# A gated broadcast on one core: gates and x swap their load queues, the first store waits for its tile alone, and one of its tokens is multiplied in one instruction

## The chip, the cores and the metric

The kernel runs on one core of a Trainium2 chip. The metric is device time in microseconds, lower is better. The engines that matter are DVE (the vector engine), ACT (the scalar engine), SP (the sync engine, which here only issues transfers) and the core's 16 DMA engines. Transfers issued by SP stand in one queue (q1 in the profile), those issued by ACT in another (q10); both are served by the same 16 DMA engines.

## The reference

```python
# x: 8 x 256 x 512 float32; gate_weights: 8 x 256 x 8 float32
gate_weights = gate_weights / (np.sum(gate_weights, axis=-1, keepdims=True) + 1e-8)
output = x[:, :, None, :] * gate_weights[:, :, :, None]     # 8 x 256 x 8 x 512
```

Every token's 512 values are written eight times, once for each expert, each time scaled by that expert's normalised gate. 4.26 MB are read, 33.55 MB are written.

## The kernel before, in words

The 2048 tokens are laid over 128 partitions, 16 tokens (numbered j = 0 to 15) on each, so that a partition's tokens are contiguous in memory. Everything that is read fits in the chip's memory: `g_all` holds all gates, `x_all` all of x. The products go to `ring`, which has ten slots of one token by eight experts (16 KB per partition), and from there to memory in five stores. `CHUNKS` lists them as (first token, tokens, first slot): two tokens, three, three, four, four.

Loads: SP issues the head of x (tokens 0 to 3, line 67), the body (tokens 4 to 12, line 69) and, after the entry barrier, the rest (tokens 13 to 15, line 73). ACT issues the gates (line 68). `issue_before_entry_barrier` moves the first three ahead of the barrier that all engines pass at the start, by placing them at the head of their engine's instructions.

Gates: four small DVE operations (lines 78 to 81) sum the gates, add the small constant, take the reciprocal and multiply, giving `gn`. ACT does a small copy first (line 76), so that its table is loaded early.

Products: `scale_one` makes one expert of one token, 512 elements per partition, on ACT (line 88) or DVE (line 90). `scale_token` makes all eight experts of a token in one DVE instruction (line 93), with x and the gates broadcast. Tokens 0 and 1 are split three experts to ACT and five to DVE, token 2 is all ACT's, token 3 two to ACT and six to DVE; of the later chunks the first token is ACT's, the others are whole tokens on DVE. Token 4 is a whole token too.

Stores: SP issues each store (line 118) once the tile's products are there. The first has one more wait, for the landing of the body load, put in by `add_manual_dep`. A slot that is used again waits for the store that read it.

Of the kernel before, what the change touches and what calls it, by code (L numbers as in the profile page):

```python
# [1 line left out]

# [4 lines left out]

SLOTS = 10
HEAD = 4
TAIL = 13  # L10
CHUNKS = ((0, 2, 0), (2, 3, 2), (5, 3, 5), (8, 4, 0), (12, 4, 6))


def issue_before_entry_barrier(nc, loads):
    names = [bi.ins.name for bi in loads]

    def move(nc):
        blocks = nc.main_func.blocks
        entry = blocks[0].instructions
        moved = []  # L20
        for block in blocks[1:]:
            for ins in list(block.instructions):
                if ins.name in names:
                    block.instructions.remove(ins)
                    moved.append(ins)
        assert sorted(i.name for i in moved) == sorted(names)
        for ins in reversed(moved):
            at = next(k for k, other in enumerate(entry) if other.engine == ins.engine)
            entry.insert(at, ins)

    nc.at_finalize(move)


@with_exitstack
def kernel(
    ctx: ExitStack,
    tc: tile.TileContext,
    x: bass.AP,
    gate_weights: bass.AP,
    out: bass.AP,  # L40
):
    nc = tc.nc
    P = 128

    B, S, D = x.shape
    E = gate_weights.shape[-1]
    J = B * S // P

    fp32 = mybir.dt.float32
    mult = mybir.AluOpType.mult  # L50

    x_v = x.flatten_outer_dims().rearrange("(p j) d -> p j d", p=P)
    g_v = gate_weights.flatten_outer_dims().rearrange("(p j) e -> p j e", p=P)
    out_v = out.rearrange("b s e d -> (b s) e d").rearrange(
        "(p j) e d -> p j e d", p=P
    )

    pool = ctx.enter_context(tc.tile_pool(name="pool", bufs=1))

    g_all = pool.tile([P, J, E], fp32)  # L60
    x_all = pool.tile([P, J, D], fp32)
    ring = pool.tile([P, SLOTS, E, D], fp32)
    gsum = pool.tile([P, J, 1], fp32)
    gn = pool.tile([P, J, E], fp32)
    warm = pool.tile([P, 1], fp32)

    first_load = nc.sync.dma_start(out=x_all[:, 0:HEAD, :], in_=x_v[:, 0:HEAD, :])  # L67
    gate_load = nc.scalar.dma_start(out=g_all, in_=g_v)
    body_load = nc.sync.dma_start(
        out=x_all[:, HEAD:TAIL, :], in_=x_v[:, HEAD:TAIL, :]  # L70
    )
    issue_before_entry_barrier(nc, [first_load, gate_load, body_load])
    nc.sync.dma_start(out=x_all[:, TAIL:J, :], in_=x_v[:, TAIL:J, :])

    nc.vector.memset(warm, 0.0)  # L75
    nc.scalar.copy(out=warm, in_=warm)  # L76

    nc.vector.reduce_sum(out=gsum, in_=g_all, axis=mybir.AxisListType.X)  # L78
    nc.vector.tensor_scalar_add(out=gsum, in0=gsum, scalar1=1e-8)  # L79
    nc.vector.reciprocal(out=gsum, in_=gsum)  # L80
    nc.vector.tensor_tensor(  # L81
        out=gn, in0=g_all, in1=gsum.to_broadcast([P, J, E]), op=mult
    )

    def scale_one(engine, j, e, slot):
        o_ap, s_ap = ring[:, slot, e, :], gn[:, j, e : e + 1]
        if engine is nc.scalar:
            nc.scalar.mul(out=o_ap, in_=x_all[:, j, :], mul=s_ap)  # L88
        else:
            nc.vector.tensor_scalar_mul(out=o_ap, in0=x_all[:, j, :], scalar1=s_ap)  # L90

    def scale_token(j, slot):
        nc.vector.tensor_tensor(  # L93
            out=ring[:, slot, :, :],
            in0=x_all[:, j : j + 1, :].to_broadcast([P, E, D]),
            in1=gn[:, j, :].unsqueeze(2).to_broadcast([P, E, D]),
            op=mult,
        )

    for j0, m, s0 in CHUNKS:  # L100
        for i in range(m):
            j, slot = j0 + i, s0 + i
            if j < 2:
                for e in range(E):
                    on_act = e < 3
                    scale_one(nc.scalar if on_act else nc.vector, j, e, slot)
            elif j == 2:
                for e in range(E):
                    scale_one(nc.scalar, j, e, slot)
            elif j == 3:  # L110
                for e in range(E):
                    scale_one(nc.scalar if e < 2 else nc.vector, j, e, slot)
            elif i == 0:
                for e in range(E):
                    scale_one(nc.scalar, j, e, slot)
            else:
                scale_token(j, slot)
        store = nc.sync.dma_start(  # L118
            out=out_v[:, j0 : j0 + m, :, :], in_=ring[:, s0 : s0 + m, :, :]
        )  # L120
        if j0 == 0:
            tc.add_manual_dep(
                store.ins,
                body_load.ins.name,
                mybir.DependencyInfo(
                    mybir.DependencyClass.Sync, mybir.DependencyReason.DATA
                ),
                reason="no store among the loads",
            )


# [1 line left out]
_INS = ['x', 'gate_weights']  # L133
_OUTS = [((8, 256, 8, 512), 'float32')]


# [23 lines left out]
```

## Time and profile before

| | us |
|---|---|
| median of 7 runs | 92.31 (92.25 to 92.43) |
| profiled execution, its own time | 92.25 |
| its span, first to last instruction | 90.5 |
| DVE busy | 46.6 |
| ACT busy | 26.3 |
| first store issued | 10.58 |
| first products begun (ACT and DVE) | 6.28 |

In the profile a row of the timeline gives start and duration in us, the engine (SPq and ACTq are the issuing sequencers), the line of the kernel, the operation, the tile written and the tiles read, a count, and in brackets the idle time before it with what ended it. A row of the groups by shape gives a count, then busy us and the mean ns of one, then the idle time before them. A row of a DMA queue gives packets, MB and the time that the packets took as a share of 16 engines over the window asked for. In the row of slices each digit is the busy share of a fortieth of the span, in tenths.

### The profile page before, as it was taken

How to read it: one execution, taken by the hardware profiler on the slowest of the kernel's cores; microseconds unless marked ns; L12 is line 12 of the kernel's file. 1: busy time of each engine (PE TensorE's matmuls, PEld its weight loads, DVE VectorE, ACT ScalarE, POOL GpSimd, SP SyncE). 2: the span in 40 equal slices, each digit the busy share in tenths (PEclk: the TensorE clock that was granted, in tenths of full speed). 3: DMA queues.
4: the chain of work that ended last, by engine and by line, in shares of the span. 5: the costliest groups of instructions: out<-in, count | busy, mean ns of one | idle time of the engine just before them, and what ended most of it. 6: DMA issues, size and time to landing. Idle time of an engine off the chain costs nothing.

```text
span 90.5 us, 140 instructions
## 1 busy us (share of the span) xinstructions
DVE 46.6 (52%) x30; ACT 26.3 (29%) x42; POOL 0.2 (0%) x4
## 2 busy tenths in 40 slices
DVE  0069999999999999999990495000000000000000
ACT  4229999995990000000000498000000000000000
POOL 0000000000000000000000000000000000000000
DMA  5999999999898889888988999999999955999990
GB/s 127 454 434 399 405 529 464 464 391 420 348 696 348 348 348 696 348 348 348 696 348 348 464 464 464 464 464 464 464 464 464 464 232 232 464 464 464 464 464 0
DMA packets 1296, 37.81 MB, mean 418 GB/s; under 512 B 144, under 2 KB 272, under 8 KB 400
## 3 DMA queue, kind: packets, MB, share of 16 engines
q1 hardware_dynamic: 1152, 37.75, 97.3%
q10 hardware_dynamic: 144, 0.07, 0.2%
HBM read 4.26 MB, written 33.55 MB: 418 GB/s over the span
## 4 chain that ended last, share of the span: by engine, by line
DMA 52%; ACT 9%; ACTq 1%; SPq 0%; issue 0%
DMA out_dram<-ring 41%; DMA x_all<-in_x_dram 11%; ACT ring L88 9%; ACTq L155 1%; SPq L67 0%; ACTq L88 0%; SPq L118 0%
## 5 line engine op out<-in xcount | busy, mean ns | idle before, releaser
L93 DVE TENSOR_TENSOR ring<-x_all,gn 128x4096 f32<-128x4096 f32 x9 | 39.2, 4419 | 3.7 <-DMA out_dram<-ring 3.7
L88 ACT ACTIVATE ring<-x_all,gn 128x512 f32<-128x512 f32 x40 | 24.8, 708 | 28.5 <-DMA out_dram<-ring 25.0
L90 DVE TENSOR_SCALAR ring<-x_all,gn 128x512 f32<-128x512 f32 x16 | 6.4, 481 | 0.0
L78 DVE TENSOR_REDUCE gsum<-g_all 128x16 f32<-128x128 f32 x1 | 0.3, 286 | 3.8 <-DMA g_all<-in_gate_weights_dram 3.8
L76 ACT ACT_TABLE_LOAD x1 | 1.3, 1283 | 1.2 <-PEq L144 1.2
L75 DVE MEMSET warm<- 128x1 f32 x1 | 0.1, 59 | 1.3 <-PEq L144 1.3
L81 DVE TENSOR_TENSOR gn<-g_all,gsum 128x128 f32<-128x128 f32 x1 | 0.3, 293 | 0.0
L80 DVE RECIPROCAL gsum<-gsum 128x16 f32<-128x16 f32 x1 | 0.3, 253 | 0.0
L76 ACT COPY warm<-warm 128x1 f32<-128x1 f32 x1 | 0.2, 191 | 0.0
L79 DVE TENSOR_SCALAR gsum<-gsum 128x16 f32<-128x16 f32 x1 | 0.2, 176 | 0.0
L144 POOL MEMSET const-bfloat16-1.0<- 128x1 bf16 x1 | 0.1, 103 | 0.0
L144 POOL MEMSET const-uint8-127<- 128x1 uint8 x1 | 0.1, 102 | 0.0
L144 POOL MEMSET const-float32-0.0<- 128x1 f32 x1 | 0.1, 100 | 0.2 <-issue 0.2
L144 POOL MEMSET const-float32-1.0<- 128x1 f32 x1 | 0.1, 99 | 0.0
## 6 DMA issues: line engine op xcount, KB each, us to landing
out_dram<-ring SPq DMA_DIRECT2D x2, 6144.0 KB, 22.3
out_dram<-ring SPq DMA_DIRECT2D x1, 4096.0 KB, 11.5
x_all<-in_x_dram SPq DMA_DIRECT2D x1, 2304.0 KB, 10.1
x_all<-in_x_dram SPq DMA_DIRECT2D x1, 1024.0 KB, 4.9
x_all<-in_x_dram SPq DMA_DIRECT2D x1, 768.0 KB, 11.1
g_all<-in_gate_weights_dram ACTq DMA_DIRECT2D x1, 64.0 KB, 5.0
out_dram<-ring SPq DMA_DIRECT2D x2, 28.2
```

Source lines behind the costliest of these rows:

```text
L75: nc.vector.memset(warm, 0.0)
L76: nc.scalar.copy(out=warm, in_=warm)
L78: nc.vector.reduce_sum(out=gsum, in_=g_all, axis=mybir.AxisListType.X)
L79: nc.vector.tensor_scalar_add(out=gsum, in0=gsum, scalar1=1e-8)
L80: nc.vector.reciprocal(out=gsum, in_=gsum)
L81: nc.vector.tensor_tensor(out=gn, in0=g_all, in1=gsum.to_broadcast([P, J, E]), op=mult)
L88: nc.scalar.mul(out=o_ap, in_=x_all[:, j, :], mul=s_ap)
L90: nc.vector.tensor_scalar_mul(out=o_ap, in0=x_all[:, j, :], scalar1=s_ap)
L93: nc.vector.tensor_tensor(out=ring[:, slot, :, :], in0=x_all[:, j : j + 1, :].to_broadcast([P, E, D]), in1=gn[:, j, :].unsqueeze(2).to_bro ...
L144: nc = _bacc.Bacc("TRN2", target_bir_lowering=False, num_devices=1)
L155: with _tile.TileContext(nc) as tc:
```

## The change

The gates are issued by SP and are its first instruction. x comes in two loads (tokens 0 to 3, tokens 4 to 15) that ACT issues; all three are ahead of the barrier. Token 0 is one whole-token multiply on DVE; token 1 is split four experts to ACT and four to DVE (before: three and five for each of both tokens). The first store no longer waits for a load, only for its tile. Products of all other tokens, the chunks and the slots are as they were. On DVE the whole-token multiply of token 0 stands ahead of the one-expert multiplies of tokens 1 and 3.

```diff
-    first_load = nc.sync.dma_start(out=x_all[:, 0:HEAD, :], in_=x_v[:, 0:HEAD, :])
-    gate_load = nc.scalar.dma_start(out=g_all, in_=g_v)
-    body_load = nc.sync.dma_start(
-        out=x_all[:, HEAD:TAIL, :], in_=x_v[:, HEAD:TAIL, :]
-    )
-    issue_before_entry_barrier(nc, [first_load, gate_load, body_load])
-    nc.sync.dma_start(out=x_all[:, TAIL:J, :], in_=x_v[:, TAIL:J, :])
+    first_load = nc.scalar.dma_start(out=x_all[:, 0:HEAD, :], in_=x_v[:, 0:HEAD, :])
+    gate_load = nc.sync.dma_start(out=g_all, in_=g_v)
+    last_load = nc.scalar.dma_start(out=x_all[:, HEAD:J, :], in_=x_v[:, HEAD:J, :])
+    issue_before_entry_barrier(nc, [first_load, gate_load, last_load])
...
-            if j < 2:
+            if j == 0:
+                scale_token(j, slot)
+            elif j == 1:
                 for e in range(E):
-                    on_act = e < 3
-                    scale_one(nc.scalar if on_act else nc.vector, j, e, slot)
+                    scale_one(nc.scalar if e < 4 else nc.vector, j, e, slot)
...
-        store = nc.sync.dma_start(
+        nc.sync.dma_start(
             out=out_v[:, j0 : j0 + m, :, :], in_=ring[:, s0 : s0 + m, :, :]
         )
-        if j0 == 0:
-            tc.add_manual_dep(
-                store.ins,
-                body_load.ins.name,
-                mybir.DependencyInfo(
-                    mybir.DependencyClass.Sync, mybir.DependencyReason.DATA
-                ),
-                reason="no store among the loads",
-            )
```

More of the change, by code (lines that the diff above doesn't have):

```diff
@@ L9 @@
 HEAD = 4
-TAIL = 13
 CHUNKS = ((0, 2, 0), (2, 3, 2), (5, 3, 5), (8, 4, 0), (12, 4, 6))
```

## The prediction

> **What bounds the kernel now.** I read the busy shares over time first, because they say whether any engine is the limit, then the chain that ended last, then the edges of the transfer stream. The page of the kernel before:
>
> ```profile
> span 90.5 us, 140 instructions
> DVE 46.6 (52%) x30; ACT 26.3 (29%) x42; POOL 0.2 (0%) x4
> ...
> DMA  5999999999898889888988999999999955999990
> ```
>
> The compute engines are half idle; the DMA engines are full from the second slice to the last but one. (The two 5s are large packets counted where they start: in the packet records the 16 engines are all occupied there.) By those records the first packet starts at 1.00 us and the last ends at 89.26 us, with no hole between. The time is thus 1.00 us of start, 88.26 us of transfer, 1.2 us until the last landing has been seen and the program ended, and 92.25 - 90.5 = 1.75 us around the span. The chain in order of time shows where this stream could break:
>
> ```profile
> 0.42 10.06 DMA x_all<-in_x_dram
> 10.49 0.02 issue
> 10.50 0.03 SPq L118
> 10.53 0.05 issue
> 10.58 11.49 DMA out_dram<-ring
> ```
>
> The first store is issued at 10.58, 0.09 us after the body of x has landed, and not because its tile is late: of the compute before it, DVE's ten multiplies end at 6.28 + 9 x 0.397 + 0.48 = 10.33 and ScalarE's six at 6.28 + 5 x 0.614 + 0.71 = 10.06. The last piece of x, issued at 1.25 us, lands 11.1 us later, at 12.35. So store packets stand in the queue before the loads run out: the first starts at 11.56, 0.98 us after its issue, and engine by engine stores follow loads (mean over the 16 engines 11.77, last 11.94). From there to the end of the last packet there are 77.37 us of stores per engine, in the mean. The change can only move the beginning: when x starts, and whether a store is ready when x ends.
>
> What feeds the first tile now, from the timeline and the groups by shape:
>
> ```profile
> 0.00 0.37 SPq L67 DMA_DIRECT2D x_all<-in_x_dram  x1
> 0.12 0.37 ACTq L68 DMA_DIRECT2D g_all<-in_gate_weights_dram  x1
> 5.13 0.29 DVE L78 TENSOR_REDUCE gsum<-g_all 128x16 f32<-128x128 f32 x1 [3.75 <-DMA g_all<-in_gate_weights_dram]
> 6.28 14.82 ACT L88 ACTIVATE ring<-x_all,gn 128x512 f32<-128x512 f32 x24 [3.54 <-DVE gn L81]
> 6.28 6.43 DVE L90 TENSOR_SCALAR ring<-x_all,gn 128x512 f32<-128x512 f32 x16
> 12.62 34.77 DVE L93 TENSOR_TENSOR ring<-x_all,gn 128x4096 f32<-128x4096 f32 x8
> ...
> L93 DVE TENSOR_TENSOR ring<-x_all,gn 128x4096 f32<-128x4096 f32 x9 | 39.2, 4419 | 3.7 <-DMA out_dram<-ring 3.7
> L90 DVE TENSOR_SCALAR ring<-x_all,gn 128x512 f32<-128x512 f32 x16 | 6.4, 481 | 0.0
> ```
>
> Spacings follow: (6.43 - 0.48) / 15 = 0.397 us for a one-expert multiply on DVE, (14.82 - 0.71) / 23 = 0.614 on ScalarE, (34.77 - 4.42) / 7 = 4.34 for a whole token at once. The gates land at 5.11 and cost 1.15 us of DVE work, so the multiplies start at 6.28 although the head of x is there at 4.93. How the gates stand in the queues, from the transfers of the first 2.5 us:
>
> ```profile
> DMA packets 45, 0.37 MB, mean 147 GB/s; under 512 B 0, under 2 KB 0, under 8 KB 0
> q1 hardware_dynamic: 45, 0.37, 58.1%
> ```
>
> Only q1, sync's queue, has moved anything: the gates (q10), issued at 0.12, have their first packet at 2.51, when most engines have done three packets of x.
>
> **The change, part by part.** *Gates first on sync's queue.* If x does not get in their way, eight packets of 512 B per engine (27 ns each) begin about 1.0 us and land around 2.5; the normalised gates are ready 1.15 us later, before the head of x. The gates then bind nothing as long as they land by 5.05 - 1.15 = 3.9. *x on ScalarE's queue.* That engine's first issue stood at 0.12, sync's at 0.00. If both queues are alike, x is 0.12 us later: head landed 4.93 + 0.12 = 5.05. Not alike, the bound above is the gates' own wait, 2.51 - 0.12 = 2.39 us to a first packet instead of 1.00, thus 1.39 more. I take the near end, because gates queued among full engines need not show the queue's own delay. *One load for two.* Per descriptor 0.686 us for 18 KB and 0.234 for 6 KB against about 0.91 for 24 KB (slope of 8 and 18 KB): 8 ns x 8 packets = 0.07 us less. ScalarE now issues two loads (0.37 + 0.42) ahead of the barrier and reaches it at about 0.96, where sync reached it at 0.84; its table load (1.28 us) then ends near 2.7, covered by the wait for x until 5.05. Sync loses two load issues, and only stores stand behind its gates.
>
> *The first tile.* DVE now does token 0 in one multiply and four experts of token 1: 4.34 + 3 x 0.397 + 0.48 = 6.01 us, against 4.05 before, so the broadcast form costs 1.96 us more on the path; ScalarE's four (2.55 us) lie beside it. From x's landing, with 0.02 us to wake: 5.07 + 6.01 + 0.09 = 11.17 for the first store's issue, against 10.58. Starting 1.21 us earlier is more than eaten up. *The wait for the body goes.* Alone it was worth 10.49 - 10.33 = 0.16 us, and nothing while loads fill the engines; what is late next is the tile.
>
> *The sum.* Loads end at 11.77 + 0.12 - 0.07 = 11.82 (mean). A store issued at 11.17 has packets 1.19 us later, at 12.36, if it is like sync's first DMA (first packets 1.00 to 1.56 us after its issue, mean 1.19). The stream starts 12.36 - 11.77 = 0.59 us later: 92.25 + 0.59 = 92.84 in the profiled execution, which lay 0.06 under the median of the runs; 92.9. The delay from issue to packet on an idle queue is bounded below by the issue itself, 0.35 us, which gives 11.52, under the loads' end, hence 92.31 + 0.05 = 92.36; for the first packet the row of 0.98 bounds it above; I take 1.0 and the spread, the only row with an idle queue.
>
> The Trainium skill, "DMA: Bandwidth & Descriptors", section "Latency and other measured facts", gives about 0.6 us to the first byte of a DMA issued by sync or ScalarE. The row here shows 1.00; by the rule the store would start at 11.77 and this change would cost nothing. The skill's "Perfetto Trace Analysis", section on the HWDGE DMA instruction, says a descriptor generator is shared by the two issuing sequencers and locked by one at a time, which speaks against putting anything ahead of x; here both first issues took 0.37 us while overlapping, so no lock wait is seen in them. By it x would wait for the gates' descriptors, toward the 1.39 us above.
>
> **Covers after that.** The second store needs token 4: 5.07 + 4.34 + 10 x 0.397 + 4.42 = 17.8, against 17.0 before; its turn comes when the first store is through, near 22. Four us of cover, and a delayed second load (landing near 12.3, needed by DVE at 13.4) has 1.1. Later stores have more. If a cover failed, the failure would be an idle stretch of that length.
>
> **The rivals.** *A, ScalarE's queue is slow to start.* All of x is up to 1.39 us later, the tile with it: 92.90 + 1.39 = 94.3 at most, 93.6 at half. For: 2.39 against 1.00. Against: the gates' place behind three packets of x on most engines can be read-ahead. *B, the gates do not get ahead.* If they alternate with x as before and land at 5.1, multiplies start at 6.26 again: store at 12.36, 1.19 us more, 94.1; with half of that 93.5. Against: they are issued 0.12 us earlier, and eight such packets take 0.22 us. *C, no gap* (the other side): packets within 11.82 - 11.17 = 0.65 us of the issue; the loads' end decides, 92.36. For: no row shows this delay for a store on an idle queue, only that it is at most 0.98 for the earliest. Against: the one DMA on an idle queue took 1.00. *D, faster*: the slow first packets are the mechanism. The 8 KB packets of the head ran up to 1.14 us where later ones take 0.31, 0.59 us per engine in all. If the gates absorb all of it, the store is issued at 11.17 - 0.59 = 10.58 and its packets start at 11.23 to 11.77 by delays of 0.65 to 1.19: between -0.54 and nothing, -0.27 in the middle, 92.04. It decides, by more than 0.18, once packets follow within 1.01 us. Against: x's addresses are touched no earlier than before.
>
> **How the numbers follow.** About 0.2% (0.18 us, the spread of the runs shown) is what the measurement can tell from no change. Forecast (gap of 0.3 to 0.9 us, 92.6 to 93.2): 0.46. A 0.17, B 0.11: slower 0.74. C 0.18 is the same. D 0.08 is faster. The range from 92.25 to 94.0 leaves out D and the outer thirds of A and B.
>
> **What would show it.** Right: a first packet of x near 1.1, gates landed before 3.9, first multiply near 5.07 released by x, first store at 11.2 released by DVE, and a hole of about half a us in the transfers near 12, nowhere else. Head landing past 5.8 would show A; a first multiply released by the gates, B; a full stream with packets within 0.65 us, C; head landing by 4.6, D. A hole behind the second store would make the whole sum wrong.

## The result, and the profile after

The changed kernel takes 92.67 us (median of 13 runs, 92.58 to 92.96) against 92.38 for the kernel before (34 runs, 92.21 to 92.59): a ratio of 1.0038, 95% interval 1.0030 to 1.0047. It is slower by 0.29 us in the medians. The forecast was slower, by 0.59, to 92.9. The profiled execution took 92.75, so it lies 0.08 above its median, while that of before (92.25) lay 0.13 under its own: of the 0.50 between the two profiled executions 0.21 are such scatter, and traces are compared below with that in mind.

The page of the changed kernel, span, engines and transfers in 40 slices:

```profile
span 91.0 us, 132 instructions
DVE 48.6 (53%) x25; ACT 25.1 (28%) x40; POOL 0.2 (0%) x4
...
DMA  4989899879899889988998999999999739999990
```

Its chain in order of time (start, us, what):

```profile
0.12 4.87 DMA x_all<-in_x_dram
...
5.09 4.43 DVE ring L89
9.52 3.96 DVE ring L86 x10
13.48 13.01 DVE ring L89 x3
...
26.56 24.85 DMA out_dram<-ring
```

Before, this chain held transfers alone up to 22 us: loads until 10.48, then the first store. Now DVE stands in it from 5.09 on, since x's landing no longer is what the first store waits for. The timeline of the beginning gives the steps:

```profile
0.00 0.38 SPq L67 DMA_DIRECT2D g_all<-in_gate_weights_dram  x1
0.12 0.37 ACTq L66 DMA_DIRECT2D x_all<-in_x_dram  x1
...
2.13 0.29 DVE L74 TENSOR_REDUCE gsum<-g_all 128x16 f32<-128x128 f32 x1 [0.60 <-DMA g_all<-in_gate_weights_dram]
...
5.08 13.58 ACT L84 ACTIVATE ring<-x_all,gn 128x512 f32<-128x512 f32 x22 [2.20 <-DMA x_all<-in_x_dram]
5.09 4.43 DVE L89 TENSOR_TENSOR ring<-x_all,gn 128x4096 f32<-128x4096 f32 x1 [1.85 <-DMA x_all<-in_x_dram]
9.43 4.05 DVE L86 TENSOR_SCALAR ring<-x_all,gn 128x512 f32<-128x512 f32 x10
11.19 15.71 SPq L115 DMA_DIRECT2D out_dram<-ring  x3
```

The gates land three us earlier than before and the multiplies are released by x at 5.09 instead of by the gates at 6.28; the first store is issued at 11.19 all the same, against 10.58. What that does to the transfers is seen in the stretch from 11.2 to 12.9 us, in which each digit is a fortieth and shows packets where they start. First the kernel before, then the changed one:

```profile
DMA  9066999399990999990000000000000000009999
...
q1 hardware_dynamic: 69, 0.91, 125.3%
```

```profile
DMA  0000000000000000000999900000000000000000
...
q1 hardware_dynamic: 16, 0.52, 71.7%
```

Before, the last pieces of x and the first of the store follow each other without a break. After, no data packet starts between 11.2 and 12.0; the 16 that then start within 0.15 us are the first store's, one for each engine. By the packet records the last load packets end at 11.41 to 11.91 (mean over the engines 11.68), the store's begin at 12.03 to 12.18 (mean 12.09): the engines stood for 0.41 us in the mean. The stores thus begin 0.32 us later than before (mean 11.77). That this hole is the change's loss is shown by the runs below, and that closing it is not enough.

### The profile page after: what moved, and what is told of

Same layout as the page of the kernel before. It is cut to its first block, busy times and chain, and to the rows that moved or that the text cites. A ratio compares the mean times of both kernels' runs of the same rounds, so it can differ in the third digit from the quotient of the medians.

```text
span 91.0 us, 132 instructions
## 1 busy us (share of the span) xinstructions
DVE 48.6 (53%) x25; ACT 25.1 (28%) x40; POOL 0.2 (0%) x4
## 4 chain that ended last, share of the span: by engine, by line
DMA 33%; DVE 24%; ACT 5%; ACTq 1%; issue 0%; DVEq 0%; SPq 0%
DMA out_dram<-ring 27%; DVE ring L89 19%; DMA x_all<-in_x_dram 5%; ACT ring L84 5%; DVE ring L86 4%; ACTq L143 1%; DVEq L89 0%; ACTq L84 0%; SPq L115 0%
## 5 line engine op out<-in xcount | busy, mean ns | idle before, releaser
L89 DVE TENSOR_TENSOR ring<-x_all,gn 128x4096 f32<-128x4096 f32 x10 | 43.6, 4421 | 5.2 <-DMA out_dram<-ring 3.3
L84 ACT ACTIVATE ring<-x_all,gn 128x512 f32<-128x512 f32 x38 | 23.6, 707 | 30.0 <-DMA out_dram<-ring 27.8
L86 DVE TENSOR_SCALAR ring<-x_all,gn 128x512 f32<-128x512 f32 x10 | 4.0, 481 | 0.0
```

What stands on the lines that cost most here:

```text
L89: nc.vector.tensor_tensor(out=ring[:, slot, :, :], in0=x_all[:, j : j + 1, :].to_broadcast([P, E, D]), in1=gn[:, j, :].unsqueeze(2).to_bro ...
```

## Experiments

Times are medians, with the kernel before on the same chip beside them, then the ratio and its 95% interval. "Theory" stands for one of the rival accounts that an expectation names; Q (two queues) and E (early store) are two of them. "Store sum" below is the time that all store packets took, per DMA engine, from the packet records.

**The first tile alone**, in the kernel before (its loads, queues and wait kept):

```diff
-            if j < 2:
+            if j == 0:
+                scale_token(j, slot)
+            elif j == 1:
                 for e in range(E):
-                    on_act = e < 3
-                    scale_one(nc.scalar if on_act else nc.vector, j, e, slot)
+                    scale_one(nc.scalar if e < 4 else nc.vector, j, e, slot)
```

> The kernel before with only the first tile changed (token 0 in one DVE multiply, token 1 four and four); its loads, queues and the store's wait for the body stay. Theory 1: the tile starts at 6.28 and is ready at 6.28 + 6.01 = 12.29, the store is issued at 12.4 and its packets start 0.9 later at 13.3, loads end at 11.77: a hole of 1.5 us, 93.9 us. Theory 2, that the tile is off the path and the queues are the cost: 92.4 us, as before.

93.96 us against 92.33, ratio 1.0178 (1.0164 to 1.0192). The waits of SP's queue now name DVE's one-expert multiplies where they named the load of x:

```profile
SPq L119 <- DVE ring L90: 10.7, 1, 10.7
```

The store was issued at 12.35, its packets began at 13.25 (mean) after loads that ended at 11.77 (mean). The slower tile is on the path as the prediction put it, and the hole of 1.48 us costs its length and 0.15 more.

**The hole closed.** Token 1 split six to ACT, two to DVE:

```diff
-                    scale_one(nc.scalar if e < 4 else nc.vector, j, e, slot)
+                    scale_one(nc.scalar if e < 6 else nc.vector, j, e, slot)
```

> The changed kernel with token 1 split six experts to ACT and two to DVE (was four and four); nothing else moves. Theory 1, the hole: the loss is the stretch of about 0.41 us between the last load packet (mean 11.68) and the first store packet (mean 12.09), set by DVE's path to the first tile. DVE then needs 4.34 + 0.40 + 0.48 = 5.22 us instead of 6.01, so the store is issued at 10.4 and its packets follow 0.9 later, at 11.3, under the loads' end: no hole, 92.67 - 0.41 = 92.26 us, at or just under the kernel before. Theory 2, the queues: x behind ScalarE's issue, or stores beside loads of another queue, cost the time; then closing the hole leaves it at 92.6 or more.

92.80 us against 92.33, 1.0055 (1.0042 to 1.0067): no faster than the change, though the store was issued at 10.20 and its packets began right behind the loads, at 11.34 to 11.70. The same stretch of 11.2 to 12.9 us as above:

```profile
DMA  0009999999090000000000000000000000000000
...
q1 hardware_dynamic: 16, 0.52, 117.2%
```

Each engine starts one store packet and none a second before 12.9. Fifteen of these first packets took 1.88 to 2.29 us, where a packet of that size takes 1.213 before; the pause is 0.78 us per engine in the mean. If each paused first and then moved its packet in 1.213, these fifteen engines went on together, at 12.2 to 12.5. Theory 1 failed: the hole was closed, and a pause of twice its size had come instead. The time is as theory 2 had it (92.6 or more), and of the two reasons it names, stores beside loads of another queue fits; that it would be a pause in the first store packets it did not say. The same with the split five and three, which issues the store later:

```diff
-                    scale_one(nc.scalar if e < 4 else nc.vector, j, e, slot)
+                    scale_one(nc.scalar if e < 5 else nc.vector, j, e, slot)
```

> The changed kernel with token 1 split five experts to ACT and three to DVE: the first store is issued near 10.75, between the 6/2 split (10.20) and the change (11.19), and at the moment of the kernel with only the queues swapped (10.68). The 6/2 split closed the hole and yet was slower: its first store packets stood 0.8 us longer than the later ones and all engines went on together near 12.33, 2.1 us after the store's issue. Theory Q, two queues: a store on SP's queue that comes up while ACT's queue still moves loads makes the engines pause until about 2.1 us after its issue; then here data flows at 12.8 and the time is 93.2 us or more. Theory E, early store: the pause comes only from standing behind loads for over a microsecond; here packets would start near 11.7, right at the loads' end, without a pause: 92.35 us.

92.85 against 92.30, 1.0055 (1.0041 to 1.0069). Store at 10.64; nine of the first packets of the store took 0.14 to 0.82 us longer than 1.213, the mean over all engines is 0.23, and the engine with the longest pause ended the kernel (last packet end 89.93, mean over the engines 89.28). Theory Q had the pause, but all engines going on at 12.8, where by the same reckoning the nine did so between 11.7 and 12.6, and the time too high (93.2 or more); theory E had no pause.

**The loads of the change alone**, with the first tile of before:

```diff
-            if j == 0:
-                scale_token(j, slot)
-            elif j == 1:
+            if j < 2:
                 for e in range(E):
-                    scale_one(nc.scalar if e < 4 else nc.vector, j, e, slot)
+                    on_act = e < 3
+                    scale_one(nc.scalar if on_act else nc.vector, j, e, slot)
```

> The changed kernel with the first tile made as before (both tokens three experts to ACT, five to DVE, no whole-token multiply): the loads of the change alone, and no wait of the store for a load. Theory 1: tile ready at 5.09 + 9 x 0.397 + 0.48 = 9.14, store issued at 9.25, packets from 10.15 on, sharing the engines with the last packets of x; no hole, 92.2 to 92.3 us as with the 6/2 split, since it can gain no more than the hole. Theory 2, stores among loads cost something: slower than the 6/2 split by 0.1 us or more, the landing of x pushed back past 13.5 and token 4 waiting for it.

92.61 against 92.33, 1.0032 (1.0019 to 1.0044). The store went out at 9.19. Here it was load packets, those starting at 10.47 to 10.97, that took up to 0.48 us longer than their usual 0.912 (0.27 per engine), and the store's first ones 0.03. Neither theory has this: theory 1 had no loss, theory 2 more than with the 6/2 split, and x landing past 13.5. Token 4 did wait for x, but only 1.1 us, until 12.55. Yet here, too, packets under way about two us after a store was issued ran long.

**The queues alone**, in the kernel before:

```diff
-    first_load = nc.sync.dma_start(out=x_all[:, 0:HEAD, :], in_=x_v[:, 0:HEAD, :])
-    gate_load = nc.scalar.dma_start(out=g_all, in_=g_v)
-    body_load = nc.sync.dma_start(
+    first_load = nc.scalar.dma_start(out=x_all[:, 0:HEAD, :], in_=x_v[:, 0:HEAD, :])
+    gate_load = nc.sync.dma_start(out=g_all, in_=g_v)
+    body_load = nc.scalar.dma_start(
...
-    nc.sync.dma_start(out=x_all[:, TAIL:J, :], in_=x_v[:, TAIL:J, :])
+    nc.scalar.dma_start(out=x_all[:, TAIL:J, :], in_=x_v[:, TAIL:J, :])
```

> The kernel before with only the queues changed: gates first on SP, the same three loads of x on ACT (two ahead of the barrier, the last after it); first tile and the store's wait for the body as before. Theory 1: the gates land near 2.1 and the head near 5.0, so the tile is ready at 9.2, but the store waits for the body (10.5) and its packets start at about 11.5, under the loads' end near 11.75: 92.3 to 92.4 us, no difference. Theory 2: the swap alone costs 0.2 us or more (92.6).

92.55 against 92.33, 1.0025 (1.0016 to 1.0034): a difference of the size that theory 2 had, where theory 1 had none. It does not lie in the span (median 90.5, as before, and no pause) but around it: 2.03 us instead of 1.80. More on that below.

**One queue for loads and store.** Three ways to have it. Only the first store of the 6/2 split on ACT, behind x's loads:

```diff
-        nc.sync.dma_start(
+        (nc.scalar if j0 == 0 else nc.sync).dma_start(
```

> The 6/2 split with only the first store issued by ACT, on the queue that holds the loads of x; the other stores stay on SP, and ACT's multiplies behind it wait up to 1.5 us. Theory Q: the pause of 0.8 us in the first store's packets is gone, stores follow loads at 11.5 to 11.7: 92.2 to 92.3 us. Theory E, or a theory that the 3 MB load is at fault: as with the 6/2 split, 92.8 us.

92.33 against 92.30, 1.0005 (0.9996 to 1.0013). Same loads, same tile, store issued at 10.27 beside 10.20; the stretch of 11.2 to 12.9:

```profile
DMA  0000999999999000000000000000000009999999
...
q10 hardware_dynamic: 46, 0.98, 134.3%
```

The second packets start from 12.6 on; every packet of this store took 1.213 us, and the pause is gone. Its span is 90.3, under that of before; again 2.03 us lie around it.

Everything on SP, in the 6/2 split:

```diff
-    first_load = nc.scalar.dma_start(out=x_all[:, 0:HEAD, :], in_=x_v[:, 0:HEAD, :])
     gate_load = nc.sync.dma_start(out=g_all, in_=g_v)
-    last_load = nc.scalar.dma_start(out=x_all[:, HEAD:J, :], in_=x_v[:, HEAD:J, :])
+    first_load = nc.sync.dma_start(out=x_all[:, 0:HEAD, :], in_=x_v[:, 0:HEAD, :])
+    last_load = nc.sync.dma_start(out=x_all[:, HEAD:J, :], in_=x_v[:, HEAD:J, :])
```

> The 6/2 split with everything on SP's queue: gates, then the two loads of x, then the stores (x is issued near 0.4 us instead of 0.12). Theory Q, two queues: no pause, because loads and store share a queue; head landed near 5.1, store issued near 10.4, stores follow loads at about 11.7: 92.2 to 92.4 us. Theory E, early store, or a theory that the one load of 3 MB is at fault: the first store packets take 2 us as with the 6/2 split, 92.8 us.

92.75 against 92.30, 1.0048 (1.0036 to 1.0060): the forecast of the time failed, yet there is no pause. x is issued behind the gates at 0.42 and its first packets come at 1.75 (mean of the first 16) instead of 1.45 with the 6/2 split; the stream starts and ends later. The stores begin at 12.00 in the mean and on the last engine at 12.37, against 11.77 and 11.94 in the kernel before. This run tells the theories apart by its trace, not by its time.

The kernel before without the store's wait:

```diff
-        store = nc.sync.dma_start(
+        nc.sync.dma_start(
             out=out_v[:, j0 : j0 + m, :, :], in_=ring[:, s0 : s0 + m, :, :]
         )
-        if j0 == 0:
-            tc.add_manual_dep(
...
-            )
```

> The kernel before without the first store's wait for the body load; nothing else. The store is issued when its tile is there, 10.33 + 0.09 = 10.42 instead of 10.58, on the queue that also holds the loads. Theory Q: nothing changes, 92.33 us (the loads fill the engines until 11.8). Theory E, early store: the store now stands 1.35 us behind loads, as with the 6/2 split; a pause of half a us or more would show, 92.8.

92.26 against 92.30, 0.9999 (0.9991 to 1.0008). Store at 10.29, no pause: on one queue an early store simply stands behind the loads.

**Smaller packets on the other queue.** The 6/2 split with x's second load cut in two:

```diff
-    last_load = nc.scalar.dma_start(out=x_all[:, HEAD:J, :], in_=x_v[:, HEAD:J, :])
-    issue_before_entry_barrier(nc, [first_load, gate_load, last_load])
+    body_load = nc.scalar.dma_start(out=x_all[:, HEAD:13, :], in_=x_v[:, HEAD:13, :])
+    last_load = nc.scalar.dma_start(out=x_all[:, 13:J, :], in_=x_v[:, 13:J, :])
+    issue_before_entry_barrier(nc, [first_load, gate_load, body_load, last_load])
```

> The 6/2 split with the second load of x cut into tokens 4 to 12 and 13 to 15 (three loads on ACT, all ahead of the barrier), first store on SP at 10.2. With only the queues swapped, a store issued at 10.68 came up beside 6 KB packets of ACT's queue and there was no pause; with one 24 KB load, issued at 10.64, nine of 16 engines paused. If the size of the packets in flight decides, there is no pause here: span near 90.3, and 92.35 us with 2.05 around it. If any load on the other queue does it, once the store is issued early enough: first store packets up to 2 us long, span 91.0, 93.05 us.

92.57 against 92.27, 1.0032 (1.0020 to 1.0045). Store at 10.25 on SP; no packet of the first store longer than 1.213. So a load on the other queue is not enough: it takes the large packets (24 KB), or that they belong to one load; these two were not separated. The span is 90.5, the time around it 2.07.

**The change with its first store on ACT** (the edit of the 6/2 split above, made in the changed kernel):

> The change (four and four) with only the first store issued by ACT, on x's queue. Theory Q: with the change itself the store's packets come after the loads have run out, so there is a hole and no pause, and moving the store to the other queue leaves the hole at 0.4 us: span 90.9 to 91.0 as with the change. The time around the span was 1.77 us in kernels with one or two transfers issued by ACT and 2.04 to 2.05 in the two with three; if the third transfer is the reason, it is 2.04 here and the time 92.9 us. If the queue matters in the change too, the span is 90.6 or less.

92.63 against 92.27, 1.0038 (1.0024 to 1.0052). As theory Q had it, the hole stays (loads end 11.57, store packets from 11.98 on, means) and with it the loss; the pause plays no part in the change itself. From the kernel of the 6/2 split with its first store on ACT this one differs by the split of token 1 alone: without the hole the stores begin at 11.56 and the span is 90.3, with it they begin at 11.98 and the span is 90.8 (90.5 for the kernel before beside both). This pair is the plainest price of the hole, 0.5 us of span. The time around the span was 1.81, though, so a third transfer on ACT is not what lengthens it.

**Two versions that beat both kernels.** x in two loads on SP, gates on ACT, the first tile of before, and no wait (taken out as above):

```diff
-    body_load = nc.sync.dma_start(
-        out=x_all[:, HEAD:TAIL, :], in_=x_v[:, HEAD:TAIL, :]
-    )
-    issue_before_entry_barrier(nc, [first_load, gate_load, body_load])
-    nc.sync.dma_start(out=x_all[:, TAIL:J, :], in_=x_v[:, TAIL:J, :])
+    last_load = nc.sync.dma_start(out=x_all[:, HEAD:J, :], in_=x_v[:, HEAD:J, :])
+    issue_before_entry_barrier(nc, [first_load, gate_load, last_load])
...
```

> The kernel before without the first store's wait and with x in two loads (tokens 0 to 3, 4 to 15) on SP, both ahead of the barrier; gates on ACT and the first tile as before. It is the version the runs point to: x first at 0.00, one queue for loads and stores, no broadcast multiply in the first tile. One DMA and 0.07 us per engine of descriptors less, nothing else: 92.2 to 92.3 us; if one load of 3 MB were itself a cost, slower than 92.4.

92.14 against 92.27, 0.9983 (0.9974 to 0.9992), span 90.3: a small gain, a little more than expected. And the 6/2 split with its first store on ACT and two multiplies fewer there:

```diff
             elif j == 3:
                 for e in range(E):
-                    scale_one(nc.scalar if e < 2 else nc.vector, j, e, slot)
+                    scale_one(nc.vector, j, e, slot)
```

> The 6/2 split with the first store on ACT, and token 3 wholly on DVE (eight one-expert multiplies, before two of them on ACT). In the kernel without that last edit the span was 90.3, 0.2 under the kernel before, but 2.03 us lay around the span instead of 1.78. The time around was long in the three kernels with 40 multiplies and three transfers on ACT, and not in one with 38 and three, nor with 40 and two. Theory L, the length of ACT's program: with 38 and three it is 1.8 here, and the time 90.3 + 1.8 = 92.1 us, level with x in two loads on SP. Otherwise it stays at 2.03: 92.33 us. The span should not move, as DVE has several us in hand before the second store.

92.11 against 92.31, 0.9976 (0.9967 to 0.9985): span 90.3 as before the edit, 1.79 around it. The time around the span is 2.03 to 2.07 in the three kernels in which ACT has 40 multiplies and three transfers, 1.76 to 1.81 in all others, this one included. That it is the length of ACT's program fits all of them; what happens there lies outside the trace.

## Why the prediction was right in direction, and where its size was off

- *Which wait ends last.* Right. The first store went from waiting for the body of x to waiting for its tile; issue forecast at 11.17, measured 11.19. Head landed 5.05 forecast, 4.99 measured; first multiply 5.07, measured 5.09; 6.01 us for the tile, as forecast.
- *Gates ahead.* Right: the first normalising operation begins at 2.13, so the gates bind nothing. In the first 2.5 us they are through, and x has moved too:

```profile
q10 hardware_dynamic: 40, 0.33, 43.8%
q1 hardware_dynamic: 144, 0.07, 9.1%
```

- *x on ACT's queue* (rivals A and B). Its first packet starts at 1.25, 1.13 us after the issue, not 2.39: the queue is not slow, and the gates' late place before was not that queue's own delay, as assumed. What held them there is not shown. Rival B fell with the gates' landing. The shared, locked descriptor generator of the Trainium skill ("Perfetto Trace Analysis", section on the HWDGE DMA instruction) left no mark here: the two issues overlap and take 0.38 and 0.37 us.
- *Loads' end*: 11.82 forecast, 11.68 measured, from errors of both signs. The engines' first packets of x start at about 1.6 us in the mean, 0.4 later than before, where 0.12 was forecast. But the 0.22 us per engine that the gates' packets take now lie mostly ahead of x and not among it, and the head's packets ran 0.34 us over their usual length in sum, not 0.59. This last is what rival D spoke of, and the sum put it at nothing: the nine kernels with gates first on SP and x on ACT show 0.29 to 0.44, the four with x first on SP 0.46 to 0.59. That the gates absorb it is not shown: with gates and then x on SP's queue it is 0.48.
- **The term that was mis-sized: from issue to packets on an idle queue.** Put at 1.19 (mean), taken from the first load; the store took 0.84 to 0.99, mean 0.90, and in the tile-only kernel 12.35 to 13.25, again 0.90. The start of the stores thus moved by 12.09 - 11.77 = 0.32, not 0.59. Taking the row of another kind of DMA, with its spread over engines, was the mistake; the nearer row, 0.98 for the first store of the kernel before, was in hand and used as a bound only. The skill's 0.6 us to the first byte ("DMA: Bandwidth & Descriptors", "Latency and other measured facts"), counted from the issue as the prediction did, is still short of it: by it the store's packets would begin at 11.79, only about 0.1 us behind the mean end of the loads, 11.68.
- *What the sum lacked.* After a hole store packets take slightly longer (medians 1.219, 1.820 and 2.422 us by size, against 1.213, 1.815 and 2.418 before): store sum 77.71 to 77.72 us in the three kernels with a hole, 77.44 to 77.54 in the nine with neither a hole nor a pause at the store. In the first three all engines start their stores within 0.15 us of each other, in the nine over 0.28 to 0.92. That they then disturb each other is a guess. Between the two profiled executions it is 0.23 us, so the last store packet ends 0.55 us later (89.81 against 89.26): 0.32 by the start and 0.23 by the slower packets. That the profiled execution, 92.75, came within 0.09 of its forecast of 92.84 is therefore luck: 0.27 too much in one term and 0.23 missing in another. By the medians the loss is 0.29, half of the 0.59.
- *Rival C* (no hole, 92.36) needed packets within 0.65 us of the issue, and the earliest came after 0.84. It also supposed that stores ready before the loads' end cost nothing. On one queue that holds; on two, with this large load, the 6/2 split took 92.80. The section "Issuing engines are not separate DMA queues" of the same page says that issuing from several engines only saves issue time; here the issuing engine mattered beyond that: between the 6/2 split and its twin with one store on ACT there are 0.47 us.

## What to carry to other kernels

In a stream of transfers that never stops, count from the first store's issue, plus the delay to its packets (0.90 us here), back to the end of the loads: a tile made in fewer instructions but more time (4.34 us for a token where eight split multiplies over two engines took half) opens a hole that nothing closes later. Of the kernels here with x on ACT and the gates ahead of it, only the one whose first store followed on time, and from x's queue, beat the kernel before (92.11), and it needed a shorter program on ACT as well; two plain loads of x on SP gave the same (92.14). And look around the span: the 6/2 split with its store on ACT and its twin with two multiplies fewer have equal spans, 90.3, and differ by 0.24 us outside it.

## What the runs showed of the hardware that was not expected

- A store on SP's queue that comes up beside 24 KB packets of ACT's queue can make the engines pause: 0.78, 0.27 and 0.23 us per engine in three kernels (stores issued at 10.20, 9.19 and 10.64), none with 6 KB packets, none on one queue. In the change, whose store was issued at 11.19 while the last 24 KB packets ran, there was none. What the engines wait for is open, as is whether the packet's size or the number of loads decides.
- An unbroken stream keeps much of the stagger that the engines have at the start of the stores, and the last engine sets the time. Starts lay 0.38 us apart before and ends 0.25; with everything on one queue 0.74 and 0.68. After the hole of the change it was 0.15 and 0.19: a hole lines the engines up again. In the 6/2 split, where one engine did not pause, ends lay 0.76 apart.
- The time around the span was 2.03 to 2.07 us in the three kernels whose ACT program has 40 multiplies and three transfers, and 1.8 again with two multiplies fewer; what causes it is not shown.
